# Where VectorE's weight sums stand in its queue: two of the four block sums of a seven-product weight step, pinned in front of or behind named splits

## The chip, the cores and the metric

The kernel runs on one NeuronCore of a Trainium2 chip. The metric is the device time of one execution in microseconds (us); lower is better. Before the change three runs took 2848.87, 2852.01 and 2852.09 us, a median of 2852.01 us.

A core has TensorE (PE in the profile, its weight loads PEld), VectorE (DVE), ScalarE (ACT), GpSimd (POOL) and SyncE (SP), each with its own instruction queue that is worked off in order, and DMA queues that SP, ACT and POOL issue to.

## The reference

A two-layer encoder trunk runs on two sequences, 512 and 256 tokens (768 rows of 1024 values in all), with shared weights in float32. Each layer is a feed-forward half step, a mixer, and a second feed-forward half step:

```
def swiglu_ffn(x, w1, w2):
    gate, up = jnp.split(x @ w1, 2, axis=-1)
    return (jax.nn.silu(gate) * up) @ w2

for li in range(DEPTH):                       # 2 layers
    x = x + 0.5 * swiglu_ffn(rmsnorm(x, norm_g[li, 0]), ffn_w1[li, 0], ffn_w2[li, 0])
    ...                                       # mixer: HGRN2 in layer 0, windowed attention in layer 1
    x = x + 0.5 * swiglu_ffn(rmsnorm(x, norm_g[li, 2]), ffn_w1[li, 1], ffn_w2[li, 1])
return rmsnorm(x, final_norm_g)
```

`w1` is 1024 by 5632 (gate and up, 2816 columns each), `w2` is 2816 by 1024. The change touches only how the weights of the four feed-forward steps are prepared.

## The kernel before, in words

**Seven products for eight.** The feed-forward weights are worked off in two-by-two blocks. A plain two-by-two block product takes eight block products; the kernel takes seven, called p1 to p7, of sums and differences of blocks. On the weight side four sums of the raw blocks a11, a12, a21, a22 are needed:

- the first, a21 + a22, written over a21, made by an accumulating DMA that POOL issues (`into`, L141);
- the third, a11 plus the original a21, in a tile of its own called s3, also by an accumulating DMA;
- the **second**, the new a21 added to a11, written over a11, by VectorE (L206);
- the **fourth**, the new a11 added to a12, written over a12, by VectorE (L210).

p1 reads the raw a11, p2 the raw a12, p4 the raw a22, p5 the first sum, p7 the third, p6 the second and p3 the fourth. So only p6 and p3 read what VectorE adds, and both come last in the order of the products.

**Splits.** Float32 weights are split in two parts, `hi` and `lo` (`split`, L199 and L200): ScalarE rounds the block to `hi`, VectorE subtracts to get `lo`. In the up blocks GpSimd does the subtraction of p5. TensorE then takes three matmuls for each pair of tiles: hi by hi, hi by lo, lo by hi.

**Up and down.** A feed-forward step has 22 blocks of 128 hidden columns. In an up block (`up_pair`, `product`, L421) the raw tiles are one gate and one up tile, each 128 x 1024 with two raw blocks in it (a11 and a12 in the gate tile, a21 and a22 in the up tile); each product is 12 matmuls of 384 columns. After four up blocks comes a down projection (`down_quad`, L479) with four raw tiles of 128 x 1024, one for each raw block; each of its seven products is 18 matmuls of 512 columns, 6 for each of three row blocks. The order of products is `UP` = p1, p7, p2, p5, p4, p6, p3 and `DOWN` = p1, p2, p5, p4, p7, p6, p3. There are 5 down projections in each of 4 feed-forward steps, 20 in all, and 80 up blocks of seven products. TensorE's own order is a little different in the down projection: the scheduler has it begin p7 (8 of its matmuls) between p5 and p4.

**What TensorE waits for in the down projection.** p2 accumulates into the three PSUM banks of p1, p4 into those of p5, p3 into those of p7. In between VectorE must read the banks once: `add_x` (L501) adds a bank, times 0.5 or -0.5, to the residual x. So p2's first matmul waits for p1's first `add_x`, p4's for p5's first.

**What VectorE does around it.** In the last up block and the first half of the down projection VectorE has, beside the splits: L444, L447 to L455 (the differences and products that finish an up block; L444 must read a bank before p3 of that block accumulates into it), L350 to L354 (`mix`, the sums of hidden activations) and L267 (the `lo` part of those activations).

**Buffers.** Raw tiles (`wr`) have 4 buffers, split tiles (`w`) 8 of 128 x 1024, s3 tiles 2. A split takes one `w` buffer in an up block and two in a down projection. `ahead` stages splits as far ahead of their products as the 8 buffers allow, and loads (`load_next`, on SP) as the 4 raw buffers come free.

**Order.** The program is written in Python and traced; a scheduler then orders each engine's queue by when it takes instructions to be ready. In `quad_steps` before the change the second sum is traced right behind p1's split and the fourth right behind p2's, with nothing that holds their place.

Of the kernel before, what the change touches and what calls it, by code (L numbers as in the profile page):

```python
# [47 lines left out]
class Trunk:  # L48
# [123 lines left out]
    def quad_steps(self, key, raws, srcs, order):  # L172
        nc = self.nc
        flat = lambda t: t.rearrange("p a b -> p (a b)")
        up = len(raws) == 2
        if up:
            a11, a12, a21, a22 = (flat(t[:, h : h + 4, :]) for t in raws for h in (0, 4))
            three = [srcs[1].rearrange("(k p) c -> p k c", p=P)[:, :4, :]]
        else:
            a11, a12, a21, a22 = (flat(t) for t in raws)  # L180
            three = [srcs[2][:, i : i + 1, :] for i in range(2)]
        s3 = []
        for i, src in enumerate(three):
            t = self.wp.tile([P, 512], F32, tag="s3", name=self.name("s3"), bufs=2)
            self.last_load = nc.sync.dma_start(t.rearrange("p (a b) -> p a b", a=src.shape[1]), src)
            self.into(t, a11[:, i * 512 : (i + 1) * 512])
            s3.append(t)
        self.into(a21, a22)

        def split(name, srcs, eng=None):  # L190
            if up:
                w = self.wtile()
                hi, lo = w[:, :512], w[:, 512:]
            else:
                hi, lo = self.wtile(), self.wtile()
            n = srcs[0].shape[-1]
            for i, src in enumerate(srcs):
                h, l = (t[:, i * n : (i + 1) * n] for t in (hi, lo))
                nc.scalar.copy(h, src)  # L199
                (eng or nc.vector).tensor_sub(l, src, h.bitcast(F32))  # L200
            view = lambda t: t.rearrange("p (a b) -> p a b", a=4 if up else 2)
            self.staged[(*key, name)] = (view(hi), view(lo), 1 if up else 2)

        def p1():
            split("p1", [a11])
            nc.vector.tensor_add(a11, a11, a21)  # L206

        def p2():
            split("p2", [a12])
            nc.vector.tensor_add(a12, a12, a11)  # L210

        steps = {
            "p1": p1,
            "p2": p2,
            "p3": lambda: split("p3", [a12]),
            "p4": lambda: split("p4", [a22]),
            "p5": lambda: split("p5", [a21], nc.gpsimd if up else None),
            "p6": lambda: split("p6", [a11]),
            "p7": lambda: split("p7", s3),
        }  # L220
        return [(1 if up else 2, steps[name]) for name in order]

    def stage_next(self):
        if not self.loaded:
# [1057 lines left out]
```

## Time and profile before

| | |
|---|---|
| median of three runs | 2852.01 us |
| the profiled execution: its time, its span | 2852.12 us, 2850.3 us |
| granted TensorE clock, mean | 0.998 |
| PE, PEld, DVE, ACT, POOL busy share | 98%, 90%, 76%, 46%, 12% |
| DMA, mean rate over the span | 102 GB/s |
| second sums (L206) in the trace | 80 of 128 x 512, 20 of 128 x 1024 |
| fourth sums (L210) in the trace | 80 of 128 x 512, 20 of 128 x 1024 |

Times are counted from the start of the span. The busy share of PE hides short waits, so the argument goes by the starts of matmuls and by the lists of waits. A row of a timeline gives start, length, engine, line, operation, tiles, shapes and a count of merged instructions; in brackets stands the idle time before it and what ended it. DVE instructions that follow each other without idle time start a little before the one ahead has ended on paper (a 1.22 us instruction is followed 1.14 us later, one of 0.68 us 0.60 us later), so a chain of them is measured from start to start.

### The profile page before, as it was taken

Reading aid. Unit: us, or ns where it says so; the run is one execution under the profiler, and the core shown is the slowest. Engines: PE = TensorE matmul, PEld = TensorE weight load, DVE = VectorE, ACT = ScalarE, POOL = GpSimd, SP = SyncE. Lnnn points to the kernel's source line nnn. Section 1 sums busy time; section 2 is a strip of 40 time slices with the busy share of each in tenths; the row PEclk is TensorE's granted clock in tenths of the full one; section 3 lists DMA queues with packets and bytes.
Section 4 is the critical chain, followed back from the end, with each engine's and each line's share of the span. In section 5 each row is a group of like instructions: output and inputs, shape, how many; then the busy total and the mean of one; then the engine's idle time right before and its main releaser. Section 6 shows DMA issues by size and latency. Waiting matters only on the chain. (4 is left out here: it accounts for less than half of the span.)

```text
span 2850.3 us, 40558 instructions
## 1 busy us (share of the span) xinstructions
PE 2796.7 (98%) x15225; PEld 2554.2 (90%) x15225; DVE 2173.2 (76%) x3750; ACT 1318.9 (46%) x2454; POOL 355.1 (12%) x402
## 2 busy tenths in 40 slices
PE   8999999999999999999999999999999899999998
PEld 8899999889899889998998998999888789989997
DVE  7788787468577658878878887887848878788877
ACT  7344443434344336434444643444458755434443
POOL 1111111000000001111111111111002211111110
PEclk9999999999999999999999999999999999999999
DMA  6554454311111133555444355545422113555443
GB/s 165 127 125 122 116 134 121 115 44 39 44 39 38 60 97 86 132 127 122 123 119 114 84 134 127 122 121 124 126 71 75 37 51 90 135 126 125 117 121 96
DMA packets 330101, 291.37 MB, mean 102 GB/s; under 512 B 11608, under 2 KB 257840, under 8 KB 329904
## 3 DMA queue, kind: packets, MB, share of 16 engines
q1 hardware_dynamic: 294064, 212.43, 25.4%
q0 software_dynamic: 31680, 62.93, 12.6%
q10 hardware_dynamic: 4160, 13.42, 1.3%
q8 instruction: 119, 1.95, 0.3%
q14 instruction: 78, 0.64, 0.1%
HBM read 216.39 MB, written 9.44 MB: 79 GB/s over the span
## 5 line engine op out<-in xcount | busy, mean ns | idle before, releaser
L421 PE MATMUL ps<-big,w 128*128 128x384 f32 x6720 | 1172.8, 334 | 3.1 <-DVE tA L444 2.9
L421 PEld LDWEIGHTS ps<-big,w 128*128 128x128 f32 x6720 | 1165.4, 188 | 8.8 <-DVE tA L444 7.2
L199 ACT CAST w<-wr 128x512 fp32r<-128x512 f32 x600 | 416.1, 707 | 722.7 <-PE ps L421 321.0
L479 PE MATMUL ps<-w,big 128*128 128x512 f32 x2520 | 586.8, 391 | 17.4 <-DVE x L501 17.4
L479 PEld LDWEIGHTS ps<-w,big 128*128 128x128 f32 x2520 | 469.4, 188 | 129.7 <-DVE x L501 17.3
L200 DVE TENSOR_TENSOR w<-wr,w 128x512 fp32r<-128x512 f32 (+1 forms) x520 | 438.1, 853 | 95.7 <-ACT w L199 87.0
L501 DVE SCALAR_TENSOR_TENSOR x<-ps,x 128x512 f32<-128x512 f32 x468 | 305.5, 682 | 20.5 <-PE ps L479 10.2
L141 POOL DMA_DIRECT2D s<-wr x120 | 105.4, 878 | 1333.4 <-DMA wr<-in_ffn_w_dram 583.0
L261 PE MATMUL ps<-w,big 128*128 128x512 f32 x624 | 249.8, 400 | 0.2
L263 PE MATMUL ps<-w,big 128*128 128x512 f32 x624 | 245.2, 393 | 2.5 <-DVE big L330 1.3
L262 PE MATMUL ps<-w,big 128*128 128x512 f32 x624 | 244.4, 392 | 0.0
L266 ACT CAST big<-tA 128x384 fp32r<-128x384 f32 x296 | 148.0, 513 | 175.0 <-DVE tA L449 72.0
L261 PE MATMUL ps<-big,w 128*128 128x384 f32 (+2 forms) x640 | 220.8, 346 | 3.3 <-ACT big L266 2.0
L262 PE MATMUL ps<-big,w 128*128 128x384 f32 (+2 forms) x640 | 216.8, 339 | 0.7 <-DVE big L267 0.5
L263 PE MATMUL ps<-big,w 128*128 128x384 f32 (+2 forms) x640 | 215.7, 337 | 0.0
L167 DVE TENSOR_TENSOR w<-wr,w 128x1024 fp32r<-128x1024 f32 x92 | 111.6, 1222 | 83.6 <-ACT w L166 59.7
L141 POOL DMA_DIRECT2D wr<-wr x100 | 87.5, 875 | 680.0 <-DVE tA L350 319.8
L267 DVE TENSOR_TENSOR big<-tA,big 128x384 fp32r<-128x384 f32 x296 | 164.2, 566 | 7.9 <-ACT big L266 4.4
L206 DVE TENSOR_TENSOR wr<-wr,wr 128x512 f32<-128x512 f32 (+1 forms) x100 | 79.3, 793 | 114.5 <-DMA wr<-wr 85.9
L166 ACT CAST w<-wr 128x1024 fp32r<-128x1024 f32 x92 | 96.6, 1052 | 120.5 <-PE ps L262 99.7
L263 PEld LDWEIGHTS ps<-w,big 128*128 128x128 f32 x624 | 117.4, 188 | 28.8 <-DVE big L330 2.0
L261 PEld LDWEIGHTS ps<-w,big 128*128 128x128 f32 x624 | 117.8, 189 | 22.3 <-issue 0.6
(170 smaller groups left out, 3317.2 us busy)
## 6 DMA issues: line engine op xcount, KB each, us to landing
wr<-in_ffn_w_dram SPq DMA_DIRECT2D x264, 512.0 KB, 3.9
s<-in_ffn_w_dram SPq DMA_DIRECT2D x120, 256.0 KB, 3.0
s<-wr POOLq DMA_DIRECT2D x120, 256.0 KB, 4.0
wr<-wr POOLq DMA_DIRECT2D x80, 256.0 KB, 4.0
wr<-in_hg_w_in_dram SPq DMA_DIRECT2D x40, 512.0 KB, 3.8
wr<-wr POOLq DMA_DIRECT2D x20, 512.0 KB, 4.6
spill<-x ACTq DMA_DIRECT2D x12, 512.0 KB, 3.0
x<-spill ACTq DMA_DIRECT2D x12, 512.0 KB, 3.3
```

Source lines behind the costliest of these rows:

```text
L141: self.nc.gpsimd.dma_start(out, src, accum_op=ALU.add)
L167: self.nc.vector.tensor_sub(lo, raw, hi.bitcast(F32))
L199: nc.scalar.copy(h, src)
L200: (eng or nc.vector).tensor_sub(l, src, h.bitcast(F32))
L261: nc.tensor.matmul(out, a[0], b[0], start=first, stop=False)
L262: nc.tensor.matmul(out, a[0], b[1], start=False, stop=False)
L263: nc.tensor.matmul(out, a[1], b[0], start=False, stop=last)
L266: self.nc.scalar.copy(hi, src)
L267: self.nc.vector.tensor_sub(lo, src, hi.bitcast(F32))
L421: self.nc.tensor.matmul(ps, a[x], b[y], start=first and k == 0 and i == 0, stop=k == 3 and i == 2, skip_group_check=True,)
L479: nc.tensor.matmul(ps, a[x], w[y], start=name == chain and kp == 0 and q == 0, stop=kp == 1 and q == 2, skip_group_check=True,)
L501: self.nc.vector.scalar_tensor_tensor(x, ps, c, x, ALU.mult, ALU.add)
```

## The change

The two sums are taken out of p1's and p2's steps. In a down projection the second sum is traced directly in front of p6's split and the fourth directly in front of p3's. In an up block the second is traced behind p5's split and the fourth behind p4's. Each sum is passed to `keep_in_program_order`, which keeps it behind whatever was traced last before it on its engine.

```
-        def p1():
-            split("p1", [a11])
-            nc.vector.tensor_add(a11, a11, a21)
-
-        def p2():
-            split("p2", [a12])
-            nc.vector.tensor_add(a12, a12, a11)
...
+        pin = self.tc.keep_in_program_order
+        add = {"second": lambda: nc.vector.tensor_add(a11, a11, a21), "fourth": lambda: nc.vector.tensor_add(a12, a12, a11)}
+        before = {} if up else {"p6": "second", "p3": "fourth"}
+        behind = {"p5": "second", "p4": "fourth"} if up else {}
+
+        def step(name):
+            if name in before:
+                pin(add[before[name]]())
+            split(name, own[name], nc.gpsimd if up and name == "p5" else None)
+            if name in behind:
+                pin(add[behind[name]]())
+
+        return [(1 if up else 2, lambda name=name: step(name)) for name in order]
```

Instructions, shapes and their number stay as they were; TensorE's order is the same. In the changed file both sums stand on line 206, and all lines behind the edit stand 4 lower (L444 is L440, L501 is L497).

VectorE's queue just ahead of the second down projection, before. `wr_1478`, `wr_1480`, `wr_1482` and `wr_1484` are its a11, a12, a21 and a22; the four L200 of 128x1024 are the splits of p1, p2, p5 and p4:

```order
L200 TENSOR_TENSOR w_1534<-wr_1478,w_1533 128x1024
L206 TENSOR_TENSOR wr_1478<-wr_1478,wr_1482 128x1024
L200 TENSOR_TENSOR w_1565<-wr_1480,w_1564 128x1024
L444 TENSOR_TENSOR tA_1519<-tA_1519,ps_1517 128x384
L210 TENSOR_TENSOR wr_1480<-wr_1480,wr_1478 128x1024
L200 TENSOR_TENSOR w_1596<-wr_1482,w_1595 128x1024
L447 TENSOR_TENSOR tA_1518<-tA_1518,ps_1515 128x384
```

And the same place now:

```order
L200 TENSOR_TENSOR w_1534<-wr_1478,w_1533 128x1024
L200 TENSOR_TENSOR w_1564<-wr_1480,w_1563 128x1024
L440 TENSOR_TENSOR tA_1519<-tA_1519,ps_1517 128x384
L200 TENSOR_TENSOR w_1594<-wr_1482,w_1593 128x1024
L443 TENSOR_TENSOR tA_1518<-tA_1518,ps_1515 128x384
```

Both sums have left this stretch; the rest stands in the same order. Some twenty-five instructions later in the same queue, inside the down projection, before (the first three rows are the `add_x` of p2, `ps_1705` to `ps_1721` are the banks of p5 and then of p4, the L200 are the splits of p6 and p3):

```order
L501 SCALAR_TENSOR_TENSOR x_94<-ps_1650,x_94 128x512
L501 SCALAR_TENSOR_TENSOR x_96<-ps_1658,x_96 128x512
L501 SCALAR_TENSOR_TENSOR x_98<-ps_1666,x_98 128x512
L200 TENSOR_TENSOR w_1702<-wr_1478,w_1701 128x1024
L501 SCALAR_TENSOR_TENSOR x_104<-ps_1705,x_104 128x512
L501 SCALAR_TENSOR_TENSOR x_106<-ps_1713,x_106 128x512
L501 SCALAR_TENSOR_TENSOR x_108<-ps_1721,x_108 128x512
L200 TENSOR_TENSOR w_1730<-wr_1480,w_1729 128x1024
L501 SCALAR_TENSOR_TENSOR x_94<-ps_1705,x_94 128x512
```

Now (the banks of p5 are `ps_1704` to `ps_1720`):

```order
L497 SCALAR_TENSOR_TENSOR x_94<-ps_1648,x_94 128x512
L497 SCALAR_TENSOR_TENSOR x_96<-ps_1656,x_96 128x512
L497 SCALAR_TENSOR_TENSOR x_98<-ps_1664,x_98 128x512
L206 TENSOR_TENSOR wr_1478<-wr_1478,wr_1482 128x1024
L497 SCALAR_TENSOR_TENSOR x_104<-ps_1704,x_104 128x512
L497 SCALAR_TENSOR_TENSOR x_106<-ps_1712,x_106 128x512
L200 TENSOR_TENSOR w_1701<-wr_1478,w_1700 128x1024
L497 SCALAR_TENSOR_TENSOR x_108<-ps_1720,x_108 128x512
L206 TENSOR_TENSOR wr_1480<-wr_1480,wr_1478 128x1024
L497 SCALAR_TENSOR_TENSOR x_94<-ps_1704,x_94 128x512
```

In front of p5's first `add_x` stands the second sum where p6's split stood; p6's split and the fourth sum come between the following `add_x`.

SP's queue at the same place, before (`wr_1733` and `wr_1735` are the gate and up tile of the next up block, `s_259_1737` and `s_262_1745` s3 tiles of the next two):

```order
L151 DMA wr_1733<-in_ffn_w_dram 128x8x128
L151 DMA wr_1735<-in_ffn_w_dram 128x8x128
L185 DMA s_259_1737<-in_ffn_w_dram 128x4x128
L185 DMA s_262_1745<-in_ffn_w_dram 128x4x128
L151 DMA wr_1741<-in_ffn_w_dram 128x8x128
```

and now:

```order
L151 DMA wr_1733<-in_ffn_w_dram 128x8x128
L185 DMA s_259_1737<-in_ffn_w_dram 128x4x128
L185 DMA s_262_1745<-in_ffn_w_dram 128x4x128
L151 DMA wr_1735<-in_ffn_w_dram 128x8x128
L151 DMA wr_1741<-in_ffn_w_dram 128x8x128
```

The load of the next up block's second raw tile goes behind the two s3 loads, because the down projection's a21 is now read last by its second sum, which comes later.

More of the change, by code (lines that the diff above doesn't have):

```diff
@@ L202, in split @@
             self.staged[(*key, name)] = (view(hi), view(lo), 1 if up else 2)
-        def p1():
-            split("p1", [a11])
-            nc.vector.tensor_add(a11, a11, a21)
-        def p2():
-            split("p2", [a12])
[L210 to L221, printed above, removed]
+        own = {"p1": [a11], "p2": [a12], "p3": [a12], "p4": [a22], "p5": [a21], "p6": [a11], "p7": s3}
+        pin = self.tc.keep_in_program_order
[9 more added lines that the diff above has]
+        return [(1 if up else 2, lambda name=name: step(name)) for name in order]
     def stage_next(self):
```

## The prediction

> **What bounds the kernel now.** First the page with its busy times and one group of weight loads (busy, mean, and idle time before them with what ended most of it), then the lists of who TensorE and VectorE wait for (us in total, times, longest):
>
> ```profile
> span 2850.3 us, 40558 instructions
> PE 2796.7 (98%) x15225; PEld 2554.2 (90%) x15225; DVE 2173.2 (76%) x3750; ACT 1318.9 (46%) x2454; POOL 355.1 (12%) x402
> ...
> L421 PEld LDWEIGHTS ps<-big,w 128*128 128x128 f32 x6720 | 1165.4, 188 | 8.8 <-DVE tA L444 7.2
> ```
>
> ```profile
> PE ps L479 <- DVE x L501: 17.4, 37, 0.5
> ...
> PE ps L421 <- DVE tA L444: 2.9, 5, 1.1
> ```
>
> ```profile
> DVE wr L206 <- DMA wr<-wr: 85.9, 15, 6.8
> DVE tA L444 <- PE ps L421: 73.0, 39, 2.1
> ...
> DVE wr L206 <- issue: 28.0, 5, 5.9
> ```
>
> TensorE has almost no idle time, so only what still shows in its row can be won. By far the most regular of its waits is that of the down projections (L479) for VectorE's `add_x` (L501): 37 in 20 down projections. VectorE, though busy only 76%, stands still 85.9 + 28.0 = 113.9 us in front of 20 second sums (15 + 5: one in each down projection, 5.7 us on average). The second row in which VectorE is named, L444 in the last up block, belongs to the same place. So I look at one down projection, the second one, which begins at 173.97. TensorE in its timeline, and an undisturbed run of matmuls of either kind (last two rows) to measure by:
>
> ```profile
> 167.71 6.42 PE L421 MATMUL ps<-big,w 128*128 128x384 f32 x34
> 173.97 4.28 PE L479 MATMUL ps<-w,big 128*128 128x512 f32 x18
> 178.77 10.26 PE L479 MATMUL ps<-w,big 128*128 128x512 f32 x44 [0.52 <-DVE x L501]
> 189.47 14.80 PE L479 MATMUL ps<-w,big 128*128 128x512 f32 x64 [0.45 <-DVE x L501]
> 204.11 2.09 PE L421 MATMUL ps<-big,w 128*128 128x384 f32 x11
> ...
> 195.73 8.55 PE L479 MATMUL ps<-w,big 128*128 128x512 f32 x37
> ...
> 206.74 26.51 PE L421 MATMUL ps<-big,w 128*128 128x384 f32 x152
> ```
>
> The mean matmul lasts 0.39 us on paper in L479 and 0.33 in L421, but the next starts sooner. From start to start it is (8.55 - 0.39) / 36 = 0.227 us in the down projection, and (26.51 - 0.33) / 151 = 0.173 us in an up block. Then p1's 18 matmuls should be followed at 173.97 + 18 x 0.227 = 178.05, and p2 begins at 178.77: 0.72 lost. The 44 matmuls of p2, p5 and the first 8 of p7 should end at 178.77 + 9.98 = 188.75; p4 begins at 189.47: 0.72 lost. In the up block the row of 34 would last 33 x 0.173 + 0.33 = 6.06 without a stall, and lasts 6.42: 0.36 lost, too short to show as a gap.
>
> Now VectorE in the same stretch, and ScalarE, POOL and SP where they meet it:
>
> ```profile
> 168.88 1.22 DVE L206 TENSOR_TENSOR wr<-wr,wr 128x1024 f32<-128x1024 f32 x1 [5.94 <-issue]
> 170.02 1.22 DVE L200 TENSOR_TENSOR w<-wr,w 128x1024 fp32r<-128x1024 f32 x1
> 171.15 0.55 DVE L444 TENSOR_TENSOR tA<-tA,ps 128x384 f32<-128x384 f32 x1
> 171.62 1.22 DVE L210 TENSOR_TENSOR wr<-wr,wr 128x1024 f32<-128x1024 f32 x1
> 172.75 1.22 DVE L200 TENSOR_TENSOR w<-wr,w 128x1024 fp32r<-128x1024 f32 x1
> 173.89 0.54 DVE L447 TENSOR_TENSOR tA<-tA,ps 128x384 f32<-128x384 f32 x1
> ...
> 177.94 0.68 DVE L501 SCALAR_TENSOR_TENSOR x<-ps,x 128x512 f32<-128x512 f32 x1
> ...
> 185.81 1.88 DVE L501 SCALAR_TENSOR_TENSOR x<-ps,x 128x512 f32<-128x512 f32 x3
> 187.60 1.21 DVE L200 TENSOR_TENSOR w<-wr,w 128x1024 fp32r<-128x1024 f32 x1
> 188.74 1.88 DVE L501 SCALAR_TENSOR_TENSOR x<-ps,x 128x512 f32<-128x512 f32 x3
> ```
>
> ```profile
> 174.00:189.50 15.50, 14.53 (x64) 11.36 (x62) 15.47 (x28) 6.57 (x11) 1.76 (x2) 1.00 0.54 136
> ```
>
> ```profile
> 168.85 1.05 ACT L199 CAST w<-wr 128x1024 fp32r<-128x1024 f32 x1 [2.90 <-DMA wr<-wr]
> 171.76 1.05 ACT L199 CAST w<-wr 128x1024 fp32r<-128x1024 f32 x1 [1.86 <-PE ps L421]
> ...
> 195.93 1.14 ACT L199 CAST w<-wr 128x512 fp32r<-128x512 f32 x2 [1.08 <-PE ps L479]
> ```
>
> ```profile
> 164.10 0.88 POOL L141 DMA_DIRECT2D wr<-wr  x1 [10.09 <-DMA wr<-in_ffn_w_dram]
> 182.03 0.89 POOL L141 DMA_DIRECT2D wr<-wr  x1 [17.05 <-DVE w L200]
> ```
>
> ```profile
> 174.00 3.49 SPq L151 DMA_DIRECT2D wr<-in_ffn_w_dram  x2
> ```
>
> This is a queue held up at its head. The second sum stands in it and waits for the accumulating DMA that POOL issued at 164.10; the split of p2, L444 and the rest stand behind it, though nothing keeps them. From 168.88 on VectorE works the heap off: in the stretch from 174.0 to 189.5 it is busy 15.47 of 15.50 us (the row of the stretch has busy times of PE, PEld, DVE, ACT and POOL, in this order). So p1's first `add_x` comes at 177.94 and p5's first at 188.74, and TensorE waits for both.
>
> **The change part by part.** *The sums leave the stretch ahead of the down projection.* The first instruction in the heap that depends on TensorE's progress is L447, which reads p6's bank of the last up block. ScalarE's cast at 171.76, released by TensorE's end of p6, dates that bank. In front of L447 there now stand only p2's split, L444 and p5's split. p5's cast began at 168.85 with the DMA's landing and ends at 169.90; the split of 1.14 ends at about 171.1. So L447 can start at about 171.75 in place of 173.89: 2.1 us earlier. L444, which came at 171.15, no longer stands behind the second sum nor behind anything that waits for the DMA; its inputs are complete when p5 of the up block is, two products of 12 x 0.173 = 2.08 us ahead of the p3 that waits for it. The 0.36 goes.
>
> From L447 to p5's first `add_x` the queue holds the same work as before, with the second sum in the place of p6's split, both 1.22 us long (rows 168.88 and 187.60). So everything in it moves up 2.1 us as long as it stays continuous: p1's first `add_x` to 175.8, done by 176.5; p5's first to 186.6, done by 187.3.
>
> TensorE without the 0.36 reaches p2 at 178.05 - 0.36 = 177.7: cover 1.2 us, the wait goes. Without p2's wait as well it reaches p4 at 188.75 - 0.36 - 0.72 = 187.7: cover 0.4 us, the wait goes, but narrowly. p6's split now stands between p5's second and third `add_x`, so the third is done at 186.6 + 0.60 + 0.60 + 1.14 + 0.68 = 189.6; it is wanted two row blocks into p4, at 187.7 + 12 x 0.227 = 190.4. No new wait. p6's and p3's splits are wanted after all of p4 and the rest of p7, 28 matmuls or 6.4 us after 187.7; p6's ends near 189.
>
> *The sum over the kernel.* 0.72 for each of the 37 waits is 27 us. The stall of 0.36 in 20 places would be 7.2; the list of waits shows 2.9 us of them as gaps, PEld 7.2 us. I take 6, nearer to the row of this stretch. Together 33 us. 2852.12 (the profiled execution's own time, 1.8 us more than its span and within 0.2 us of the median) less 33 is 2819.
>
> *The up blocks' sums.* 80 second and 80 fourth sums of 0.68 us move a few places back in VectorE's queue. They still stand ahead of the splits that read them, and those are staged seven products (7 x 2.08 = 14.6 us) ahead. In front of L444 there was the fourth sum and is now the second, the same length; 39 times VectorE waits there for TensorE, so it is ahead anyway. I take nothing for them; without that cover one sum a block would show, 80 x 0.68 = 54 us, which the 2.9 us that L444 now costs TensorE in all speak against.
>
> *The raw tile that is freed later.* The second sum in the down projection is the last reader of a21, whose buffer the next up block's second raw tile takes. That load is the second in SP's row at 174.00, issued at its end, about 177.1; it now waits for the sum's end near 186.7. The list of DMA issues has their times to landing (last column) for such a load, for the accumulating DMA of an up block and for that of a down projection:
>
> ```profile
> wr<-in_ffn_w_dram SPq DMA_DIRECT2D x264, 512.0 KB, 3.9
> ...
> wr<-wr POOLq DMA_DIRECT2D x80, 256.0 KB, 4.0
> ...
> wr<-wr POOLq DMA_DIRECT2D x20, 512.0 KB, 4.6
> ```
>
> 186.7 + 3.9 + 4.0 = about 195, an estimate. Before it was there 4.0 after POOL's row at 182.03, by 186.0. Its readers are p5's cast on ScalarE, the second cast of the row at 195.93, and the up block's second sum, behind p2's split, which can't be ahead of the first. Both move up with TensorE, by 0.36 + 0.72 + 0.72 = 1.8 us, to 194 or 195, so the DMA comes just in time or costs ScalarE and VectorE up to 1 us. TensorE reads that p5 only in its fourth product of the next up block, at 204.11 - 1.8 + 3 x 2.08 = 208.5, and the next thing it needs from VectorE's queue behind the sum is p4's split, one product later. Cost zero; the cover is some 10 us.
>
> A rule speaks against this part. The accumulating DMA is issued by POOL at about 190.7, into a stretch where VectorE is busy. The POOL row at 182.03 lies in such a stretch (15.47 of 15.50 us) and took 0.89 us; the one at 164.10, while VectorE stood still, took 0.88. The Trainium skill, "SBUF — State Buffer", section "SBUF: two separate sides", says that a DMA from GpSimd's queue can starve because its descriptors can't be written while VectorE holds the port the two share, and gives 620 ns alone against 3100 ns beside a VectorE copy. By its figures the landing would slip 2.5 us, an estimate, to 197.5; the sum would still be 33 us, but a quarter of the cover is gone, and the last rival below would have 0.08 in place of 0.04. The two rows show no such slip.
>
> **The rivals.** *p4's wait stays.* The cover there is 0.4 us, the smallest, and the sum stands directly in front of the `add_x`. A few idle tenths in the chain behind L447 (L453 needs the last up block's p3, the `add_x` p1's matmuls) would use it up. For it: in front of p5's `add_x` stands as much work as before. Against: the chain has 2.1 us of lead and loses only what is idle. In full it gives back 20 x 0.72 = 14.4 us: 2819 + 14.4 = 2833.
>
> *The change does nothing:* p5's split stands in the same queue and waits, through its cast, for the same DMA (the cast's row at 168.85), so VectorE stands still there instead. Then 2852. Against: that split ends at 171.1, before TensorE hands over p6's bank; and L444 stands ahead of it.
>
> *Slower: the late raw tile.* The next up block's second sum, in VectorE's queue behind p2's split, holds up everything behind it until the accumulating DMA has landed: the `add_x` of p6 and p3, later L444. It decides once the landing comes past the 10 us of cover, at about 205, 10 us later than the estimate; each us beyond costs 20 us, and past 206.7 the 33 are used up. At 208 it would be 2819 + 3 x 20 = 2879. For it: the chain of sum, load, accumulation is new. Against: it needs 7.9 us of DMA to become 18, while the longest wait of any second sum for its DMA is 6.8.
>
> **How the numbers follow.** The forecast, 2819, has 0.76; p4's wait stays, 0.12; nothing, 0.08; slower, 0.04. About 0.2% (5.7 us) is what a measurement of this kernel can tell from no change. Faster holds the first two: 0.88; within 0.2% 0.08; slower 0.04. The forecast's own range goes down to 2812 (7.2 in place of 6 for L444, 20 slow restarts of some 0.1 us behind the waits, and the 3.2 us by which the runs before differ) and up to 2825; with p4's wait to 2834. So 2812 to 2834.
>
> **What would show it.** In the profile after, VectorE should have no idle time in front of the sums of 128x1024, and stand still for the DMA only in front of p5's split, with L447 starting when p6's bank is there. TensorE's list of waits should have lost L479 for L501 (right: under 3 us; p4's wait stays: about 8 us in 20 waits) and L421 for L444. A down projection should last 126 x 0.227 = 28.6 us from its first matmul to the next up block's, not 204.11 - 173.97 = 30.1. The forecast is wrong if those waits are gone and the time has not fallen by 20 us or more, or if a wait of L421 for a split or of L206 for its DMA shows up in the up block after a down projection.

## The result and the profile after

The changed kernel takes 2818.15 us (median of 4 runs, 2815.39 to 2819.91) against 2851.95 us (4 runs, 2848.87 to 2852.09) for the kernel before: a ratio of 0.9883, 95% interval 0.9866 to 0.9900. The profiled execution took 2817.06 us, 35.1 us less than that of before.

The page of the kernel after: its span, its busy times and the weight loads and matmuls of the up blocks and of the down projections.

```profile
span 2815.3 us, 40571 instructions
PE 2782.9 (99%) x15225; PEld 2559.2 (91%) x15225; DVE 2182.1 (78%) x3750; ACT 1324.4 (47%) x2454; POOL 368.8 (13%) x402
...
L417 PEld LDWEIGHTS ps<-big,w 128*128 128x128 f32 x6720 | 1165.9, 188 | 2.3 <-ACT tA L434 0.7
...
L475 PE MATMUL ps<-w,big 128*128 128x512 f32 x2520 | 575.3, 389 | 0.0
```

The matmuls of the down projections have no idle time left in front of them (0.0 in the last row), and the weight loads of the up blocks 2.3 us in place of 8.8. Whom TensorE waits for, as one list: what leads it now has nothing to do with the seven-product steps, and the only row of theirs is the last, one wait.

```profile
PE ps L111 <- DMA tB<-in_hg_g_norm_dram: 7.3, 1, 7.3
...
PE ps L417 <- ACT tA L434: 0.4, 1, 0.4
```

Whom VectorE waits for. The 20 waits of the second sums for the DMA are gone from this list; of the sums (L206) there is one wait of 0.4 us left, in an up block. The first row of the list is now the splits' wait for ScalarE's cast, which was 90.0 us before.

```profile
DVE w L200 <- ACT w L199: 125.9, 101, 2.6
```

The second down projection again, TensorE first. It begins at 171.87 and is one unbroken row of 126 matmuls; the next up block begins 28.6 us later, where it was 30.1.

```profile
171.87 28.76 PE L475 MATMUL ps<-w,big 128*128 128x512 f32 x126
200.47 4.87 PE L417 MATMUL ps<-big,w 128*128 128x384 f32 x27
```

VectorE ahead of it and in its first half:

```profile
165.82 0.56 DVE L440 TENSOR_TENSOR tA<-tA,ps 128x384 f32<-128x384 f32 x1 [0.80 <-PE ps L417]
168.70 1.23 DVE L200 TENSOR_TENSOR w<-wr,w 128x1024 fp32r<-128x1024 f32 x1 [2.32 <-ACT w L199]
169.98 0.55 DVE L443 TENSOR_TENSOR tA<-tA,ps 128x384 f32<-128x384 f32 x1
...
174.19 0.68 DVE L497 SCALAR_TENSOR_TENSOR x<-ps,x 128x512 f32<-128x512 f32 x1
...
183.83 1.22 DVE L206 TENSOR_TENSOR wr<-wr,wr 128x1024 f32<-128x1024 f32 x1
184.96 1.28 DVE L497 SCALAR_TENSOR_TENSOR x<-ps,x 128x512 f32<-128x512 f32 x2
```

VectorE still waits for the same DMA, through ScalarE's cast of p5 (168.70), but L440 (L444 before) is done by then, and behind the wait there is only the one split. L443 (L447 before) begins 1.89 us ahead of the down projection; before it was 0.08 us.

The same stretch with the other engines: the later load of the next up block's second raw tile on SP, the accumulating DMA on POOL, the first reader of what it lands, and POOL's own split beside VectorE's sum.

```profile
185.08 6.97 SPq L151 DMA_DIRECT2D wr<-in_ffn_w_dram  x3
...
189.59 0.87 POOL L141 DMA_DIRECT2D wr<-wr  x1 [6.82 <-DVE wr L206]
...
194.81 0.62 ACT L199 CAST w<-wr 128x512 fp32r<-128x512 f32 x1 [1.91 <-DMA wr<-wr]
...
195.52 1.49 POOL L200 TENSOR_TENSOR w<-wr,w 128x512 fp32r<-128x512 f32 x1 [0.74 <-ACT w L199]
195.77 1.79 DVE L206 TENSOR_TENSOR wr<-wr,wr 128x512 f32<-128x512 f32 x1
```

Where the time went can be summed over all matmuls of a trace, as the excess of each start-to-start distance over 0.227 us in the down projections and 0.173 in the up blocks. Before, the excess was 27.4 us in the down projections (13.1 at p2, 14.2 at p4) and 6.6 us in the up blocks, 33.9 together; after, it is 0.0 and 0.7. The 0.7 is one wait for ScalarE's copy (L434), at 59 us, which the trace of before does not have. The sums differ by 33.3 of the 35.1 us by which the profiled executions differ. "Excess" below is this sum.

### The profile page after: what moved, and what is told of

Same layout as the page of the kernel before. It is cut to its first block, busy times and chain, and to the rows that moved or that the text cites. A ratio compares the mean times of both kernels' runs of the same rounds, so it can differ in the third digit from the quotient of the medians.

```text
span 2815.3 us, 40571 instructions
## 1 busy us (share of the span) xinstructions
PE 2782.9 (99%) x15225; PEld 2559.2 (91%) x15225; DVE 2182.1 (78%) x3750; ACT 1324.4 (47%) x2454; POOL 368.8 (13%) x402
## 4 chain that ended last, share of the span: by engine, by line
PE 95%; DVE 2%; ACT 2%; POOL 0%; issue 0%; DMA 0%; DVEq 0%; SPq 0%; ACTq 0%; POOLq 0%
PE ps L417 41%; PE ps L475 20%; PE ps L259 8%; PE ps L258 8%; PE ps L257 8%; PE ps L667 3%; PE ps L761 1%; PE ps L319 1%; PE ps L737 1%; PE ps L1140 1%; ACT big L1118 0%; PE ps L1102 0%; PE ps L1153 0%; PE ps L1103 0%; PE ps L906 0%; PE ps L1152 0%
## 5 line engine op out<-in xcount | busy, mean ns | idle before, releaser
L417 PE MATMUL ps<-big,w 128*128 128x384 f32 x6720 | 1169.5, 334 | 0.4 <-ACT tA L434 0.4
L417 PEld LDWEIGHTS ps<-big,w 128*128 128x128 f32 x6720 | 1165.9, 188 | 2.3 <-ACT tA L434 0.7
L475 PE MATMUL ps<-w,big 128*128 128x512 f32 x2520 | 575.3, 389 | 0.0
L475 PEld LDWEIGHTS ps<-w,big 128*128 128x128 f32 x2520 | 472.8, 188 | 97.4
L200 DVE TENSOR_TENSOR w<-wr,w 128x512 fp32r<-128x512 f32 (+1 forms) x520 | 435.1, 840 | 145.7 <-ACT w L199 124.2
L497 DVE SCALAR_TENSOR_TENSOR x<-ps,x 128x512 f32<-128x512 f32 x468 | 301.9, 681 | 8.8 <-PE ps L259 8.5
L200 POOL TENSOR_TENSOR w<-wr,w 128x512 fp32r<-128x512 f32 x80 | 133.6, 1670 | 160.0 <-ACT w L199 160.0
```

Of the source, the lines that this page charges most:

```text
L417: self.nc.tensor.matmul(ps, a[x], b[y], start=first and k == 0 and i == 0, stop=k == 3 and i == 2, skip_group_check=True,)
L475: nc.tensor.matmul(ps, a[x], w[y], start=name == chain and kp == 0 and q == 0, stop=kp == 1 and q == 2, skip_group_check=True,)
L497: self.nc.vector.scalar_tensor_tensor(x, ps, c, x, ALU.mult, ALU.add)
```

## The experiments

Two theories say why the sums cost TensorE time where they stood. The **work theory**: VectorE's wait for the DMA is itself free, and TensorE pays for the work that stands in VectorE's queue between the DMA's landing and the `add_x` that TensorE needs; two sums of 1.14 us are taken out of that. The **wait theory**: what costs is that VectorE stands still for the DMA with its whole queue behind it, so it is the wait that has to go. A third question is what part the up blocks' sums have, and a fourth how much cover the late raw tile has. Each ratio is against runs of the kernel before on the same chip (medians 2850.05 to 2852.43 us).

**The down projection alone, the up blocks alone.** In the first kernel only the down projections' sums are pinned at their new places, and the up blocks' are traced as before, free; in the second the other way round.

```
-        pin = self.tc.keep_in_program_order
+        pin = (lambda i: i) if up else self.tc.keep_in_program_order
-        behind = {"p5": "second", "p4": "fourth"} if up else {}
+        behind = {"p1": "second", "p2": "fourth"} if up else {}
```

> The sums are moved and pinned in the down projections alone; in the up blocks they are traced behind p1's and p2's splits, unpinned, as before. Work theory (what paid is that 2 x 1.14 us of sums no longer stand between the DMA's landing and the add_x that TensorE waits for, and that L444 no longer stands behind the waiting sum): 2818 us, within 4 us of the changed kernel. Wait theory (what paid is that VectorE no longer stands still for the DMA with its whole queue behind it, whatever work the sums are): 2818 as well. If the up blocks' sums had a share in the gain: above 2825.

> The sums are moved and pinned in the up blocks alone; in the down projections they stand as before. Work theory and wait theory: 2852 us, no change. If the up blocks' sums had a share in the gain: below 2845.

The down projections alone: 2819.03 us, ratio 0.9892 (0.9877 to 0.9907). The up blocks alone: 2851.18 us, ratio 1.0005 (0.9996 to 1.0014). So the time comes from the down projections. In the list of TensorE's waits of the up-only kernel both rows of before are back:

```profile
PE ps L475 <- DVE x L497: 17.2, 37, 0.5
...
PE ps L417 <- DVE tA L440: 2.6, 5, 1.0
```

The down-only trace is not quite that of the changed kernel, though: 8 of its 20 down projections have a new excess, all in front of p3, 3.6 us together and up to 1.6 us in one. In another, with 0.8 us, VectorE:

```profile
1324.17 0.69 DVE L206 TENSOR_TENSOR wr<-wr,wr 128x512 f32<-128x512 f32 x1 [2.19 <-issue]
1324.78 1.88 DVE L497 SCALAR_TENSOR_TENSOR x<-ps,x 128x512 f32<-128x512 f32 x3
```

and TensorE, which begins p3 at 1325.61:

```profile
1316.74 8.32 PE L475 MATMUL ps<-w,big 128*128 128x512 f32 x36
1325.61 2.77 PE L475 MATMUL ps<-w,big 128*128 128x512 f32 x11 [0.55 <-ACT w L199]
```

The sum at 1324.17 is the next up block's second sum. Unpinned it stands in front of p7's three `add_x` and waits there for the accumulating DMA that the change has made late; p3 of the down projection, which needs the first of these, waits with it. (The brackets name ScalarE, but p3 begins 0.15 us after the first of these `add_x` has ended, at 1325.46.) In the changed kernel this sum stands further back. So the up blocks' half of the change removes nothing of the old cost, but in the trace it keeps 3.6 us from coming back. The two kernels' times can't be told apart.

**Only the fourth sum moved.** In the down projection the second sum goes back behind p1's split, pinned; the fourth stays in front of p3's. TensorE's order is that of the changed kernel.

```
-        before = {} if up else {"p6": "second", "p3": "fourth"}
-        behind = {"p5": "second", "p4": "fourth"} if up else {}
+        before = {} if up else {"p3": "fourth"}
+        behind = {"p5": "second", "p4": "fourth"} if up else {"p1": "second"}
```

> In the down projections the second sum stays early, behind p1's split, where it waits for the DMA; the fourth alone goes in front of p3's split. Up blocks as in the changed kernel. Work theory: 1.14 us less work ahead of p1's first add_x, so L447 comes at about 172.75 in place of 173.89, p2's wait goes (17 x 0.72 = 12 us), p4's falls from 0.72 to about 0.35 (20 x 0.37 = 7 us), the stall at L444 stays: 2852 - 19 = 2833 us. Wait theory: VectorE still stands still for 5.7 us with everything behind it, so 2852.

2828.98 us, ratio 0.9928 (0.9915 to 0.9940); the work theory had 2833, the wait theory 2852. What VectorE waits for in front of the second sums, and its timeline:

```profile
DVE wr L206 <- DMA wr<-wr: 79.8, 15, 6.0
...
DVE wr L206 <- issue: 28.2, 5, 6.1
```

```profile
169.43 1.23 DVE L206 TENSOR_TENSOR wr<-wr,wr 128x1024 f32<-128x1024 f32 x1 [6.14 <-issue]
...
171.71 0.55 DVE L440 TENSOR_TENSOR tA<-tA,ps 128x384 f32<-128x384 f32 x1
...
173.31 0.55 DVE L443 TENSOR_TENSOR tA<-tA,ps 128x384 f32<-128x384 f32 x1
```

and TensorE:

```profile
172.31 2.37 PE L417 MATMUL ps<-big,w 128*128 128x384 f32 x12 [0.82 <-DVE tA L440]
174.52 29.19 PE L475 MATMUL ps<-w,big 128*128 128x512 f32 x126
```

VectorE stands still for the DMA nearly as long as ever, 108.0 us in all against 113.9 before and 6.14 us in this place, and with p2's split, L440, p5's split and L443 behind it. Yet 21 us are won: one sum fewer behind the wait, L443 1.21 us ahead of the down projection in place of 0.08, no excess at p2 and 6.7 us at p4. That is against the wait theory, and the clearest test of it here. What this kernel does keep is the excess at L440, 5.9 of the 6.6 us in its up blocks: L440 has nothing to do with the DMA and stands behind it.

**Both sums behind p5's split.** Here nothing that waits for the DMA stands ahead of p5's split.

```
-        before = {} if up else {"p6": "second", "p3": "fourth"}
-        behind = {"p5": "second", "p4": "fourth"} if up else {}
+        before = {}
+        behind = {"p5": "second", "p4": "fourth"} if up else {"p5": "both"}
```

("both" issues the second and then the fourth.)

> In the down projections both sums are pinned behind p5's split: p2's split and L444 go ahead of them and no sum waits for the DMA, but both sums still stand ahead of p1's first add_x. Up blocks as in the changed kernel. Work theory: only the stall at L444 goes (6 us), p2's and p4's waits stay: 2846 us, between 2842 and 2850. Wait theory: nothing waits at the head of the queue any more, so 2818 to 2825.

2827.50 us, ratio 0.9921 (0.9907 to 0.9934): in neither range, and nearer to the wait theory's 2825 than to the work theory's 2842. It still decides nothing, because the scheduler had also changed TensorE's order. One matmul of p5 goes ahead of p2 and the rest of p5 is interleaved, and 14 matmuls of p7 in place of 8 stand between p5 and p4, which is 6 x 0.227 = 1.4 us more cover for p4. The excess is 0.7 in the up blocks (L440 ahead of the wait), 3.1 at p2, none at p4, and 4.9 at p5, where there was none and whose cause was not looked into.

**Both sums in front of p5's split.** The same question with TensorE's order that of the changed kernel ("both" as above).

```
-        before = {} if up else {"p6": "second", "p3": "fourth"}
+        before = {} if up else {"p5": "both"}
```

> In the down projection both sums stand together in front of p5's split, behind p2's split and L440 and ahead of L443 and p1's first add_x; TensorE's order is the same as in the changed kernel. VectorE again stands still in front of the second sum until the accumulating DMA has landed, but p2's split and L440 (1.14 + 0.68 us) are done by then. Work theory (what TensorE pays is the work queued between the landing and the add_x): L443 starts some 0.4 us later than in the changed kernel (estimated -1.5 us from the down's first matmul, against -1.88 there and -0.08 before), which p2's cover just takes, and L440 is not late: 2818 to 2824 us. Wait theory (VectorE's standstill with the queue behind it is what costs): nearly all is lost, 2846 to 2852 us.

2823.94 us, ratio 0.9899 (0.9884 to 0.9914). VectorE:

```profile
167.21 0.56 DVE L440 TENSOR_TENSOR tA<-tA,ps 128x384 f32<-128x384 f32 x1 [0.80 <-PE ps L417]
169.13 2.49 DVE L206 TENSOR_TENSOR wr<-wr,wr 128x1024 f32<-128x1024 f32 x2 [1.37 <-DMA wr<-wr]
...
172.67 0.55 DVE L443 TENSOR_TENSOR tA<-tA,ps 128x384 f32<-128x384 f32 x1
```

The second sum waits for the DMA at the head of the queue again, and 28 us of the gain stay, because p2's split and L440 now stand ahead of the wait: behind it stands 1.14 + 0.47 us less than before, and the up blocks' excess is 0.7. L443 begins at 172.67, only 0.58 us ahead of the down projection (173.25) and not the 1.5 of the expectation: the DMA let the sums begin 4.1 us ahead of it, where they began 5.1 us ahead before. p4's cover is gone in many down projections, 5.9 us of excess, and at p2 there are 1.1. TensorE in this one, p4 at 188.27:

```profile
173.25 14.55 PE L475 MATMUL ps<-w,big 128*128 128x512 f32 x62
188.27 14.82 PE L475 MATMUL ps<-w,big 128*128 128x512 f32 x64 [0.46 <-DVE x L497]
```

The wait theory's 2846 us is far off, but this is a weaker test of it than the expectation has it: p2's split and L440 fill most of the time that VectorE stood still, and in front of the sums only 12.2 us of standstill are left in all, against 113.9 before.

The trace has a better one. The landing differs from one down projection to the next, and TensorE's loss at p2 and p4 follows L443's lead on the down projection: none where the lead is 1.9 us, 0.3 us at 1.3, 1.0 at 0.57 (the second one) and 1.15 at 0.43 (the one that begins at 2478.01). Before the change, the down projection that begins at 1135.12 had a lead of 0.44 and lost 1.12. The second sum and L447 of that one, then the sums and L443 of the one at 2478.01:

```profile
1129.67 1.22 DVE L206 TENSOR_TENSOR wr<-wr,wr 128x1024 f32<-128x1024 f32 x1 [5.21 <-DMA wr<-wr]
...
1134.68 0.55 DVE L447 TENSOR_TENSOR tA<-tA,ps 128x384 f32<-128x384 f32 x1
```

```profile
2474.04 2.49 DVE L206 TENSOR_TENSOR wr<-wr,wr 128x1024 f32<-128x1024 f32 x2 [1.52 <-DMA wr<-wr]
...
2477.58 0.55 DVE L443 TENSOR_TENSOR tA<-tA,ps 128x384 f32<-128x384 f32 x1
```

With the same lead the loss is the same within 0.03 us, though VectorE stood still for 5.21 us in the one and 1.52 in the other. So what TensorE pays here goes by when L443 starts, which the landing and the work behind it decide.

**The places alone, without the pin.** The steps issue their sums where the change has them, and nothing is pinned.

```
-        pin = self.tc.keep_in_program_order
+        pin = lambda i: i
```

> The steps issue their sums at the changed places, but nothing is pinned, so that the scheduler is free to place them. It puts the second sum back behind p1's split and the fourth behind L440, as before. Both theories: 2852 us (2848 to 2855), p2's and p4's waits at L475 back (about 17 us in 37) and L440's too. If the place in the program alone did it: 2818 us.

2853.92 us, ratio 1.0006 (0.9996 to 1.0015). The list of TensorE's waits has `PE ps L475 <- DVE x L497: 17.2, 38, 0.5` and `PE ps L417 <- DVE tA L440: 2.5, 6, 0.9`, as before. The scheduler puts the down projections' sums back where they were, so without the pin the new places do nothing.

**Both sums between p2's and p5's `add_x`.** A price by hand for a sum that is put one place too early.

```
-        before = {} if up else {"p6": "second", "p3": "fourth"}
+        before = {} if up else {"p6": "both"}
```

> In the down projection the second sum stays in front of p6's split, and the fourth sum moves up to stand right behind p5's first add_x, followed by p6's split and only then p5's second add_x, which p4's second part waits for on TensorE. In the changed kernel p5's first add_x ends at 185.65 us in the second down and p4's second part begins on TensorE at 187.32: fourth sum and p6's split of 1.14 us each put p5's second add_x at 187.9 to 188.5. TensorE's order changes by 7 matmuls of p7 that go ahead of p5's second part, which leaves p4's place. Work theory: a wait of 1.2 us in each of 20 downs, 2842 us (2836 to 2846). Wait theory (no transfer is waited for at either place): 2818 us, no wait.

2817.19 us, ratio 0.9886 (0.9869 to 0.9902): the time of the changed kernel. VectorE does what was said:

```profile
185.00 0.68 DVE L497 SCALAR_TENSOR_TENSOR x<-ps,x 128x512 f32<-128x512 f32 x1
185.61 1.21 DVE L206 TENSOR_TENSOR wr<-wr,wr 128x1024 f32<-128x1024 f32 x1
186.74 1.22 DVE L200 TENSOR_TENSOR w<-wr,w 128x1024 fp32r<-128x1024 f32 x1
187.88 1.28 DVE L497 SCALAR_TENSOR_TENSOR x<-ps,x 128x512 f32<-128x512 f32 x2
```

and TensorE waits for nothing:

```profile
171.91 28.76 PE L475 MATMUL ps<-w,big 128*128 128x512 f32 x126
```

I had misread where the 7 matmuls of p7 went: not ahead of p5's second part but between p4's first and second part. They put p4's second part off by 7 x 0.227 = 1.6 us, more than the 1.2 us that the sum cost. So this kernel, too, says nothing against or for a theory; it shows that the scheduler moves TensorE's order to suit VectorE's, and that a wait worked out in a fixed order may not come.

**How late the raw tile may be.** One, two or three (the number in `range`; the line that makes the scratch is not shown) extra DMAs stand on POOL's queue ahead of the accumulating DMA of the up block behind each down projection, 20 places. They copy a21 to a scratch in DRAM that nothing reads; the accumulating DMA writes a21 and so waits for them. These files' lines are a little lower: sums L210, `add_x` L501, products L421 and L479, the PSUM copy L434 is L438.

```
+        if up and key[1] >= 4 and key[1] % 4 == 0:
+            for _ in range(1):
+                nc.gpsimd.dma_start(self.hold, a21)
         self.into(a21, a22)
```

> One more DMA of 256 KB (the tile a21 written to a scratch in DRAM) stands on POOL's queue ahead of the accumulating DMA of every fourth up block, 20 times: work added, no result of it used. It makes that tile land about 4 us later (194.7 to about 199 us in the second down). The late tile (the rival that ended slower) was given some 10 us of cover: 2818 us (2815 to 2822), no new wait on TensorE. If the cover is under 4 us: more than 1 us each, 2840 us or over.

> Two extra DMAs ahead of the accumulating one, at the same 20 places. One made the tile land 4.1 us later and TensorE waited for nothing; three made it land 18.5 us later (213.2 us) and TensorE stood still for 6.0 us, so that the cover comes to about 12.5 us. Two should land it some 11 us later, at about 206 us. Cover of 12.5 us: no new wait of more than 0.5 us, 2818 to 2828 us, and no stretch of slow matmuls. Cover of 10 us, as the prediction had it: a wait of about 1 us each, 2838 us or over. If the slow matmuls of the run with three (320 ns for 12 to 15 of them behind each gap) come with any late tile and not with TensorE's standstill, they are seen here too.

> Three more such DMAs ahead of it, 20 times: the tile lands some 12 us later (about 206.7 us, where TensorE reaches the product p5 at 206.7 us, and ScalarE's cast of 1.9 us and POOL's split of about 1.5 us still have to run). With a cover of 10 us: a wait of 2 to 4 us at p5 of the next up block, 20 times, 2858 to 2898 us. If the DMAs overlap so that it lands under 8 us later, or the cover is longer: 2818 us.

One: 2823.06 us, ratio 0.9895 (0.9880 to 0.9910), a little over the expected range. Two: 2899.17 us, ratio 1.0171 (1.0156 to 1.0186). Three: 2974.76 us, ratio 1.0425 (1.0407 to 1.0442); both cost far more than expected. The cover of 12.5 us that I had read from the run with three is wrong: I had compared times of day of two traces, though in that run an earlier late tile had already moved the second down projection by 7.8 us. From the down projection's own start the first reader of the tile comes at 194.81 - 171.87 = 22.9 us in the changed kernel, and with three at 213.20 - 179.71 = 33.5. With two, all engines around the place (the down projection began at 174.93):

```profile
203.69 4.35 PE L421 MATMUL ps<-big,w 128*128 128x384 f32 x24
...
206.80 0.69 DVE L210 TENSOR_TENSOR wr<-wr,wr 128x512 f32<-128x512 f32 x1 [7.01 <-DMA wr<-wr]
...
209.39 0.68 DVE L210 TENSOR_TENSOR wr<-wr 128x512 f32<-128x512 f32 x1
...
210.16 1.14 ACT L203 CAST w<-wr 128x512 fp32r<-128x512 f32 x2 [1.56 <-DVE wr L210]
...
211.72 0.47 ACT L438 COPY tA<-ps 128x384 f32<-128x384 f32 x1
...
212.25 1.01 PE L421 MATMUL ps<-big,w 128*128 128x384 f32 x2 [4.20 <-ACT tA L438]
```

This chain is how a late tile reaches TensorE: landing, second sum, fourth sum, ScalarE's cast of what the fourth sum wrote, and behind that cast in ScalarE's queue the copy that empties a PSUM bank; TensorE's third product of the up block, 24 matmuls in, writes that bank again. From the first reader to TensorE's restart it takes 212.25 - 206.80 = 5.45 us. TensorE wants the bank 28.6 + 24 x 0.173 = 32.75 us behind the down projection's start, so the first reader must come by 32.75 - 5.45 = 27.3, and it comes at 22.9: the cover is 4.4 us. With one extra DMA it comes at 198.81 - 171.70 = 27.1, just in time; the excess behind the down projections is 0.3 us in that place and 2.2 us in all 20. In the list of VectorE's waits of that run stands

```profile
DVE wr L210 <- issue: 56.8, 20, 3.5
```

These are 20 new waits of 2.8 us on average at the head of VectorE's queue, for 2.2 us of excess. That fits the work theory: a wait is free while the work behind it still comes in time.

Three extra DMAs also show a second price. The list of TensorE's waits has

```profile
PE ps L421 <- ACT tA L438: 109.3, 21, 6.3
```

which is 109 us; the profiled execution is 159 us longer than that of the changed kernel. The rest lies behind each standstill. The stretches of the gap at the second down projection, and of the 4 us behind it (busy times of PE, PEld, DVE, ACT, POOL; then the granted clock):

```profile
212.50:218.50 6.00, 0.17 (x1) 0.00 (x0) 4.69 (x7) 3.62 (x8) 1.26 (x1) 0.90 0.25 68
218.50:222.50 4.00, 3.88 (x12) 3.88 (x13) 2.16 (x4) 0.97 (x3) 0.88 (x1) 0.50 0.88 245
```

Right behind the gap the granted clock is 0.50, and the matmuls follow each other at 0.320 us in place of 0.173. The gaps (112 us) and the slow stretches (47 us, 2.3 us each) make 159 us. With two the gaps are 62.6 us and the slow stretches 23.5, together 86.1, where the profiled execution is 85.1 us longer. With one extra DMA the tile is late by 4.2 us, TensorE doesn't stand still, and no matmul is slow: the standstill brings them, not the late tile.

No kernel here beats the changed one: it has next to no excess left in the seven-product steps.

## Why the prediction was right

By its own steps:

- *L447 starts 2.1 us earlier.* Right. The prediction had it 1.9 us ahead of the down projection (171.75, with TensorE 0.36 earlier at 173.61); it begins 1.89 us ahead.
- *p2's wait goes, cover 1.2 us.* Right. p1's first `add_x` ends at 174.87, p2 begins at 171.87 + 18 x 0.227 = 175.96: cover 1.1 us.
- *p4's wait goes, narrowly, cover 0.4 us.* Right. The first of the pair at 184.96 ends at about 185.65, p4 begins at 171.87 + 62 x 0.227 = 185.94: cover 0.3 us, and no down projection has an excess there. Both covers are smaller by the hand-over, which the prediction left out: before, p2 began at 178.77, 0.15 us after the `add_x` had ended (177.94 + 0.68). So about 0.15 us was left at p4. The rival that p4's wait stays was that near; with both sums in front of p5's split it is what happens, and puts 5.9 us back.
- *37 waits of 0.72 us, 27 us.* The excess of 27.4 us is gone. *L444, 6 us.* It was 6.6, in 15 of the 20 places and from 0.1 to 1.3 us, and is gone; the 0.7 left in the up blocks is the wait for ScalarE. The 6 was a choice between two sizes, and that it fits so well is partly luck.
- *The up blocks' sums cost and bring nothing.* Right for the price; but the half of the change for which the prediction took nothing is what keeps a late second sum away from p7's `add_x`, 3.6 us by the trace.
- *VectorE stands still at p5's split instead, without harm.* Right: 2.32 us in the row at 168.70. The reason was the work theory's, and it was tested where the wait stays at the sum. Only L440's part, 6 of the 33 us, comes of standing behind the wait at all. The other 27 are the amount of work between the landing and L443, and whose work it is matters little: with the fourth sum taken out 20.7 us of the 27.4 come back, with p2's split and L440 taken out in place of the sums 20.4.
- *The rule against it.* By the figures of the Trainium skill, "SBUF — State Buffer", section "SBUF: two separate sides", the accumulating DMA issued beside a busy VectorE would have landed 2.5 us later, an estimate. This trace doesn't bear it out: POOL's row at 189.59 took 0.87 us, with VectorE busy around it, and from that row's start to the landing the 20 DMAs at this place take 5.2 us (median), against 4.8 before.
- *The late raw tile: cover some 10 us, decides at about 205.* This step failed, though the forecast didn't depend on it: the cover is 4.4 us. Counted from the down projection's start, the prediction put the landing at 194.6 - 173.61 = 21.0 us, and the first reader came at 22.9. That both stand near 195 in time of the span is luck: the first down projection's gain had moved the second one to 171.87, 1.7 us ahead of where the prediction took it to begin. The sum was short by the 0.7 us from the load's landing (188.9) to POOL's row, and by 1.1 us for the accumulating DMA, which landed 5.1 us after the start of POOL's row, where the sum had 4.0. The need was wrong by more: it was put 31.4 us behind the start, and is 27.3. The prediction took TensorE's own reading of p5 for the first need, and went on only through VectorE's queue. The first need is a PSUM bank whose copy stands in ScalarE's queue behind the cast of the fourth sum's result. The rival's price, 20 us for each us beyond the cover, was right for the gaps at the second down projection (4.6 us beyond with two, 6.2 with three, for gaps of 4.4 and 6.1), and left out the slow matmuls behind them, 23.5 to 47 us.

Open: the profiled executions differ by 1.8 us more than the excess accounts for, and the runs of a kernel differ by more than that; what of it is a cost was not tried.

## What to carry to other kernels

A wait at the head of an in-order queue is not a price by itself: count the work that stands between its end and the instruction that the bounding engine needs, and move what is not needed out of that stretch, or ahead of the wait. When a change makes a transfer later, follow the landing through every in-order queue, those of engines that seem idle included, to the first thing that the bounding engine lacks, and count from an event that both traces share. Where a scheduler sets the order, compare all engines' orders before a variant is read as a test of one move: two of the variants here moved TensorE's as well, and neither told the theories apart.

## What the runs showed of the hardware

TensorE's standstill can cost more than its length. Behind gaps of 4.7 to 6.5 us the matmuls of 384 columns ran at 0.320 us in place of 0.173 in 20 of 20 cases, 1.4 to 2.9 us lost each time; behind gaps of 1.5 to 4.5 us in 13 of 20, about 1.7 us lost each time but one (2.7). The Trainium skill, "TensorE: Matmul & The Clock Gate", section "Part 1: The HAM clock gate (the "warmup" mystery)", has the clock halved after an idle window of about 3.4 us, a window that runs on whatever the kernel does, and free again after about as long a busy one. The half clock (0.50 above) and the length agree: in these traces the granted clock changes only on a grid of 3.41 us, and is low for one or two of its windows. The idle window doesn't quite: TensorE need not be idle for all of it.

The length of the gap does not decide: one of 2.0 us was followed by slow matmuls and one of 3.6 us was not. What goes with the slow matmuls is how much of one window of that grid stood idle. Of the 40 gaps, all that left a window idle for 63% or more were followed by half clock, and none that left every window idle for 46% or less. Three left one idle for 52 or 53%, and one of them was followed by it. In the run with two extra DMAs the gap of 3.6 us lies across two windows, and the row of the one that it left more idle is the first here. The gap of 2.0 us lies within a single window, the second row, and the third row is the window behind it. TensorE's busy time stands behind the length, the granted clock third from the end:

```profile
1183.85:1187.26 3.41, 1.64 (x9) 1.64 (x10) 3.41 (x7) 2.62 (x6) 0.00 (x0) 1.00 0.52 154
...
1692.44:1695.85 3.41, 1.60 (x10) 1.28 (x9) 3.41 (x7) 2.93 (x6) 0.00 (x0) 1.00 0.52 154
1695.85:1699.26 3.41, 3.41 (x13) 3.41 (x12) 2.17 (x4) 1.00 (x2) 0.88 (x1) 0.50 0.73 199
```

A split on POOL and a sum on VectorE at the same moment can stretch the sum: 1.79 us at 195.77, beside POOL's row at 195.52. In the trace of the changed kernel 15 of the 160 sums of 128x512 took 1.78 or 1.79 us, and all 15 began while a split ran on POOL. The 136 that began beside none took 0.67 to 0.69. Nine began while POOL's row of a split was open and took no longer; those rows of POOL lasted 2.8 to 4.4 us, in place of 1.3 to 1.7 beside the 15.
